# Feed-forwards of a hybrid decoder layer by Strassen's seven products

## The chip, the cores and the metric

One core of one Trainium2 chip runs the whole program. The metric is the device time of one execution in microseconds, the median of several runs. Lower is better.

## The reference

One layer of a decoder on 1024 prompt tokens and 64 sample tokens (8 sequences of 8), 1024 features wide, all in float32:

```python
def swiglu(x, w_in, w_out):                       # w_in 1024 x 5632, w_out 2816 x 1024
    gu = x @ w_in
    g, u = gu[..., :D_FF], gu[..., D_FF:]         # D_FF = 2816
    return (jax.nn.silu(g) * u) @ w_out

def layer(x, ...):
    x = x + 0.5 * swiglu(rmsnorm(x, norm_ffn1), ffn1_w_in, ffn1_w_out)
    mix, ... = token_mixing(rmsnorm(x, norm_mix), ...)
    x = x + mix
    x = x + 0.5 * swiglu(rmsnorm(x, norm_ffn2), ffn2_w_in, ffn2_w_out)
    return x, ...
# and a last rmsnorm over the features
```

The token mixing (a pooling branch and a state-space branch with their gates) is untouched by the change, apart from the buffers that it shares with the feed-forwards.

## The kernel before, in words

**Layout.** Everything is feature-major: a tile has 128 features on the partitions and tokens along the free dimension. The tokens are worked on in two parts, called halves: half 0 has 512 prompt tokens, half 1 has 512 prompt and 64 sample tokens, 576 together. A PSUM bank holds 512 float32 numbers, so half 1 is computed in two pieces of 288 columns.

**Precision.** Products run in the rounded format fp32r. Both operands are split into a rounded part (hi) and the exact remainder (lo), and each 128 x 128 block of weights takes part in three passes: hi x hi, hi x lo, lo x hi. `load_w` (lines 239 to 250) loads 512 columns of weights (tile `wraw`), rounds them on ScalarE (`wh`, line 248) and subtracts on VectorE (`wl`, line 249). `products` and `dense` run the three passes over all row blocks; line 140 is the one matmul line of all helpers.

**Feed-forward** (`ffn`). 22 hidden tiles of 128 features, in blocks of 3, 4, 4, 4, 4, 3. For a hidden tile, `dense` makes the gate part (PSUM tile `pg`) and the other part (`pu`) from 8 row blocks each; they are multiplied and split into hi and lo (`hb`, `hs`). After each block its hidden tiles are multiplied with the second weight (`po`) and added to the residual `x` in SBUF (line 431). The first block is done half by half, and so is the end of the last block. In the first feed-forward the products use x times the gain; the norm's factors (`rstd`) are multiplied onto the results (line 364), so that no product waits for them. In the second, `norm_split` makes the normalized operands ahead.

**Loading x** (`load_x`). Blocks of 128 tokens arrive token-major, are turned on TensorE against an identity (`ptx`, line 144), copied out of PSUM (line 466) and split.

**Order.** The kernel is written as a stream of dense products into which chains of small steps (norms, the state-space chunks, the final norm) are woven by an estimate of TensorE time (`tick`, `start`, `later`). The tile framework then orders each engine's instructions by priority and readiness, and gives out slots of the buffer pools. `hp[0]` raises the priority of the weights' splits. Loads and stores are issued from SyncE's queue (SP).

**Buffers.** One pool holds 58 slots of 128 x 576 (`act`), 3 of four times that size (`big`), 4 raw weight tiles and 4 each of `wh` and `wl`; 8 PSUM banks are shared by dense products (4) and all else (4).

**Between the feed-forwards** lies the mixing, half by half, which ends with the product `pwo` and, for half 0, a spill of x to DRAM. After the second feed-forward `final_head` and `final` turn x back to token-major, in two groups (six blocks of tokens, then three), and write the outputs.

Of the kernel before, what the change touches and what calls it, by code (L numbers as in the profile page):

```python
# [14 lines left out]
P = 128  # L15
# [19 lines left out]
FF_BLOCKS = (3, 4, 4, 4, 4, 3)   # hidden tiles per block of an FFN  # L35
N_ACT, N_BIG, N_PD = 58, 3, 4   # buffers: activation slots, 4-tile slots, PSUM banks of products
N_RAW, N_W = 4, 4   # weights as loaded, and split
# [12 lines left out]
X1_AT = 0.0  # L50
CONST_AT = 60.0
HP, HP_ST = 40, 0    # priorities of the weights' split and of the state update
N_PRE = 3            # weights ahead of x
# [3 lines left out]
def tile_hybrid_pool_ssd_macaron(  # L57
# [15 lines left out]
    pp = ctx.enter_context(tc.tile_pool(name="psum", bufs=8, space=bass.MemoryType.PSUM))  # L73
# [10 lines left out]

    def big(dt=F32, name="b"):
        return sp.tile([P, 4, 576], dt, tag="big", bufs=N_BIG, name=nm(name))

    def small(shape, name="s", bufs=2, dt=F32):
        return sp.tile(list(shape), dt, tag=name, bufs=bufs, name=nm(name))

    def psum(tag="ps", name="ps"):
        return pp.tile([P, 512], F32, tag=tag, bufs=N_PD if tag == "pd" else 8 - N_PD, name=nm(name))

# [1 line left out]
    # Chains of small steps (generators that yield how much TensorE time should pass before  # L95
    # their next step) are woven into the stream of dense products by TensorE time.
# [42 lines left out]
    def mm(out, lhsT, rhs, start=True, stop=True):  # L139
        T.matmul(out, lhsT, rhs, start=start, stop=stop)  # L140
        pe[0] += max(out.free_size(), 64) / 2400.0 * (1 if rhs.dtype == F32R else 4)
# [16 lines left out]
    # per-feature vectors arrive as rows and are turned into per-partition columns on PE  # L158
# [42 lines left out]
    xdtp = [cp.tile([P, 4, 2, P], F32, tag=f"xdtp{i}", name=f"xdtp{i}") for i in range(2)]  # L201
# [4 lines left out]
    def load_consts():  # L206
        """Constants that the mixing phase needs."""
# [11 lines left out]
        for t in xdtp:  # L219
            G.memset(t, 0.0)  # L220
# [42 lines left out]
    def dense(w, rk0, nk, c0, xs, tag="pd", name="pd"):  # L263
        """PSUM pieces of sum_k w[rk0+k, c0:c0+128]^T x[k]; xs: list of (half, hi, lo)."""
        out = banks(xs, tag, name)
        for kb in range(0, nk, 4):
            n4 = min(4, nk - kb)
            wh, wl = load_w(w, rk0 + kb, n4, c0)
            for kk in range(n4):
                products(out, wh, wl, kk, slice(0, P), xs, kb + kk, nk)  # L270
                tick()
        return out

    def dense2(w, rk0, c0, xs, tags=("pd", "pd"), name="pd"):
        """The same for two 128-column blocks of two 128-row blocks of w, one after the other."""
# [8 lines left out]
    def split(src, hi, lo, scale=1.0):  # L284
        """hi = f32r(src*scale), lo = src*scale - hi (exact)."""
# [17 lines left out]
    def rstd(tiles, h, count, out, pace=1.0):  # L303
        """Chain that fills out with rsqrt(mean(x^2)+eps) of feature-major x, on all partitions."""
# [17 lines left out]
        sm = small((P, 3, 5), "rsm", 2)  # L322
# [21 lines left out]
    def norm_split(xt, h, gi, out, pace=1.0):  # L344
        """Chain that fills out with the hi/lo parts of rmsnorm(x) of one half."""
# [25 lines left out]
    def h_tiles(nb):  # L371
        """hi and lo tiles of a block's hidden features: the big slots first, then the others."""
        room = []
        for _ in range(N_BIG):
            t = big(F32R, "hb")
            room += [t[:, j, :] for j in range(4)]
        while len(room) < 4 * nb:
            room.append(act((P, 576), F32R, "hs"))
        out = []
        for h in HALVES:  # L380
            t = [[room.pop(0)[:, : NTOK[h]] for _ in range(nb)] for _ in range(2)]
            out.append((h, t[0], t[1]))
        return out

    def ffn(xt, xs, wi, wo, before, after, rs=None, half=None, ends=((0,), (1,))):
# [3 lines left out]
        blocks, b0 = [], 0  # L389
        for nb in FF_BLOCKS:  # L390
            blocks.append((b0, nb))
            b0 += nb
        for i, (b0, nb) in enumerate(blocks):
            hp = h_tiles(nb)
            for grp in ((0,), (1,)) if i == 0 else (HALVES,):
                if i == 0:
                    before(grp[0])
                gx = [xs[h] for h in grp]
                for j in range(nb):
                    ff = b0 + j  # L400
                    first = rs is not None and i == 0 and j == 0
                    pg = dense(wi, 0, KD, ff * P, gx, "pd", "pg")
                    if first:
                        pu = dense(wi, 0, KD, FF + ff * P, gx, "ps", "pu")
                    sg = []
                    for h, pts in zip(grp, pg):
                        g_ = act((P, NTOK[h]), name="g")
                        if rs:
                            scaled(g_, pts, h, rs(h))
                            S.activation(g_, g_, AF.Silu)  # L410
                        else:
                            func(g_, pts, h, AF.Silu)
                        sg.append(g_)
                    if not first:
                        pu = dense(wi, 0, KD, FF + ff * P, gx, "ps", "pu")
                    for h, pts, g_ in zip(grp, pu, sg):
                        if rs:
                            u_ = act((P, NTOK[h]), name="u")
                            scaled(u_, pts, h, rs(h))
                            V.tensor_tensor(g_, g_, u_, op=ALU.mult)  # L420
                        else:
                            scaled(g_, pts, h, g_)
                        split(g_, hp[h][1][j], hp[h][2][j])
            last = i == len(blocks) - 1
            for gi, grp in enumerate(ends if last else (HALVES,)):
                for m in range(KD):
                    po = dense(wo, b0, nb, m * P, [(p, *hp[HALF_OF[p]][1:]) for p in grp], ("pd", "ps")[m % 2], "po")
                    for p, pts in zip(grp, po):
                        x_ = xt[HALF_OF[p]][m]
                        for pt, (a, b) in zip(pts, PIECES[p]):  # L430
                            V.scalar_tensor_tensor(x_[:, a:b], pt[:, : b - a], 0.5, x_[:, a:b],  # L431
                                                   op0=ALU.mult, op1=ALU.add)
                    if last and half and m == KD // 2 - 1:
                        half(gi)
                if last:
                    after(gi)

# [1 line left out]
    xt = [None, None]  # L439
    xs = [None, None]  # L440
# [820 lines left out]
```

## Time and profile before

| what | value |
|---|---|
| median of 3 runs | 3076.58 us (3070.76 to 3079.87) |
| profiled execution, first to last instruction | 3076.2 us |
| instructions | 46,636, of them 18,600 matmuls |
| TensorE (PE) | 3024.0 us busy, 98% |
| VectorE (DVE) | 1624.1 us, 53% |
| ScalarE (ACT) | 1028.7 us, 33% |
| GpSimd (POOL) | 56.4 us, 2% |
| DMA traffic | 261.10 MB, mean 85 GB/s |

PEld is TensorE's loading of weights, which runs beside its products. A stage's row has its window and length, then busy time and count of PE, PEld, DVE, ACT and POOL, then the granted TensorE clock (1.00 is full speed), the share of the DMA engines and GB/s. A row of the chain of waits has start, length, what ran, and how many in a row. A group's row has line, engine, operation, tiles and shapes with the count, then busy time, mean duration in ns, and the idle time of the engine before them with what ended it.

### The profile page before, as it was taken

How to read it: one execution, taken by the hardware profiler on the slowest of the kernel's cores; microseconds unless marked ns; L12 is line 12 of the kernel's file. 1: busy time of each engine (PE TensorE's matmuls, PEld its weight loads, DVE VectorE, ACT ScalarE, POOL GpSimd, SP SyncE). 2: the span in 40 equal slices, each digit the busy share in tenths (PEclk: the TensorE clock that was granted, in tenths of full speed). 3: DMA queues.
4: the chain of work that ended last, by engine and by line, in shares of the span. 5: the costliest groups of instructions: out<-in, count | busy, mean ns of one | idle time of the engine just before them, and what ended most of it. 6: DMA issues, size and time to landing. Idle time of an engine off the chain costs nothing.

```text
span 3076.2 us, 46636 instructions
## 1 busy us (share of the span) xinstructions
PE 3024.0 (98%) x18600; PEld 2750.7 (89%) x18600; DVE 1624.1 (53%) x3331; ACT 1028.7 (33%) x1967; POOL 56.4 (2%) x170
## 2 busy tenths in 40 slices
PE   6999999999999999999999999999999999999998
PEld 5999999999888888888999989999999999999997
DVE  5533333333673897777726886977773222322225
ACT  4221212121343665434425554543442212111113
POOL 0000000000000000000001110100000000000000
PEclk8999999999999999999999999999999999999999
DMA  4211111111434333435333434244432111111112
GB/s 132 67 45 45 45 45 45 45 45 43 130 97 124 113 103 92 117 117 183 91 102 95 123 104 119 88 139 124 145 113 64 44 45 45 45 45 45 45 41 98
DMA packets 439262, 261.10 MB, mean 85 GB/s; under 512 B 21795, under 2 KB 412066, under 8 KB 439036
## 3 DMA queue, kind: packets, MB, share of 16 engines
q1 hardware_dynamic: 439028, 258.11, 28.8%
q8 instruction: 146, 2.39, 0.3%
q14 instruction: 72, 0.59, 0.1%
q10 hardware_dynamic: 16, 0.00, 0.0%
HBM read 232.31 MB, written 25.97 MB: 84 GB/s over the span
## 4 chain that ended last, share of the span: by engine, by line
PE 92%; DVE 4%; DMA 2%; ACT 1%; issue 1%; SPq 0%; POOL 0%; ACTq 0%; DVEq 0%; POOLq 0%
PE pg L140 22%; PE pu L140 20%; PE po L140 17%; PE pc L140 8%; PE pz L140 6%; PE pso L140 5%; PE pwo L140 3%; PE pbp L140 3%; PE pyd L140 2%; PE pyos L140 1%; PE pst L140 1%; DMA bsel<-in_bsel_dram 1%; PE pyo L140 1%; PE pgm L140 1%; DVE wl L249 1%
## 5 line engine op out<-in xcount | busy, mean ns | idle before, releaser
L248 ACT ACTIVATE wh<-wraw 128x512 fp32r<-128x512 f32 (+1 forms) x708 | 440.2, 623 | 1643.8 <-PE pg L140 423.7
L249 DVE TENSOR_TENSOR wl<-wraw,wh 128x512 fp32r<-128x512 f32 (+1 forms) x708 | 479.1, 679 | 651.5 <-ACT wh L248 642.0
L140 PE MATMUL pg<-hi,wh 128*128 128x288 f32 (+1 forms) x1440 | 349.3, 331 | 15.4 <-ACT wh L248 15.4
L140 PE MATMUL po<-hb,wh 128*128 128x288 f32 (+2 forms) x1600 | 348.1, 339 | 0.0
L140 PE MATMUL pg<-lo,wh 128*128 128x288 f32 (+1 forms) x1440 | 346.3, 329 | 0.4 <-DVE lo L290 0.4
L140 PE MATMUL pg<-hi,wl 128*128 128x288 f32 (+1 forms) x1440 | 345.7, 328 | 0.0
L140 PE MATMUL pu<-hi,wh 128*128 128x288 f32 (+1 forms) x1248 | 293.9, 329 | 0.1
L140 PE MATMUL pu<-hi,wl 128*128 128x288 f32 (+1 forms) x1248 | 292.3, 328 | 0.0
L140 PE MATMUL pu<-lo,wh 128*128 128x288 f32 (+1 forms) x1248 | 292.2, 327 | 0.0
L140 PEld LDWEIGHTS pg<-hi,wh 128*128 128x128 f32 x1440 | 245.4, 189 | 38.0 <-ACT wh L248 16.3
L140 PEld LDWEIGHTS po<-hb,wh 128*128 128x128 f32 x1600 | 255.8, 188 | 19.6 <-ACT hb L286 0.3
L140 PEld LDWEIGHTS pg<-lo,wh 128*128 128x128 f32 x1440 | 245.3, 189 | 21.2 <-DVE lo L290 1.1
L140 PEld LDWEIGHTS pg<-hi,wl 128*128 128x128 f32 x1440 | 245.1, 189 | 20.7 <-DVE wl L249 0.4
L140 PE MATMUL po<-hb,wl 128*128 128x288 f32 (+3 forms) x1056 | 240.4, 328 | 0.0
L140 PEld LDWEIGHTS pu<-hi,wh 128*128 128x128 f32 x1248 | 211.8, 188 | 18.6 <-ACT wh L248 0.5
L140 PEld LDWEIGHTS pu<-hi,wl 128*128 128x128 f32 x1248 | 211.7, 188 | 17.7
L140 PEld LDWEIGHTS pu<-lo,wh 128*128 128x128 f32 x1248 | 211.7, 188 | 17.5
L140 PEld LDWEIGHTS po<-hb,wl 128*128 128x128 f32 x1056 | 178.6, 188 | 15.1
L431 DVE SCALAR_TENSOR_TENSOR x<-po,x 128x288 f32<-128x288 f32 (+3 forms) x240 | 108.7, 497 | 135.2 <-PE po L140 135.0
L140 PE MATMUL pc<-hi,wh 128*128 128x288 f32 (+1 forms) x576 | 162.8, 335 | 0.6 <-ACT craw L529 0.6
L140 PE MATMUL pc<-hi,wl 128*128 128x288 f32 (+1 forms) x576 | 159.7, 329 | 0.0
L140 PE MATMUL pc<-lo,wh 128*128 128x288 f32 (+1 forms) x576 | 158.6, 329 | 0.0
(283 smaller groups left out, 4608.6 us busy)
## 6 DMA issues: line engine op xcount, KB each, us to landing
wraw<-in_w_in_dram SPq DMA_DIRECT2D x260, 256.0 KB
wraw<-in_ffn_w_in_dram SPq DMA_DIRECT2D x200, 256.0 KB
wraw<-in_ffn_w_out_dram SPq DMA_DIRECT2D x64, 256.0 KB
ab<-acsd SPq DMA_DIRECT2D x64, 256.0 KB
wraw<-in_ssd_w_out_dram SPq DMA_DIRECT2D x64, 256.0 KB
wraw<-in_ffn_w_out_dram SPq DMA_DIRECT2D x48, 192.0 KB
wraw<-in_pool_w_out_dram SPq DMA_DIRECT2D x32, 256.0 KB
wraw<-in_w_o_dram SPq DMA_DIRECT2D x32, 256.0 KB
```

The costliest lines, as they stand in the source:

```text
L140: T.matmul(out, lhsT, rhs, start=start, stop=stop)
L248: S.activation(wh, raw, AF.Copy)
L249: V.tensor_tensor(wl, raw, wh.bitcast(F32), op=ALU.subtract)
L431: V.scalar_tensor_tensor(x_[:, a:b], pt[:, : b - a], 0.5, x_[:, a:b], op0=ALU.mult, op1=ALU.add)
```

## The change

The change touches both feed-forwards and what surrounds them.

**Seven products.** The weights of one hidden tile (gate and other part, each 8 row blocks) are taken as a 2 x 2 matrix of blocks: upper and lower four row blocks, gate and other columns. The inputs are taken in two by features (tiles 0 to 3 and 4 to 7) and two by tokens: columns 0 to n and n to 2n of a half, with n = 256 in half 0 and 288 in half 1. The form used is Winograd's variant of Strassen's: seven block products from four sums of weights (s1 to s4) and four of inputs. Seven input tiles per pair are kept, each holding its hi part in columns 0 to n and its lo part in n to 2n. The second product pairs hidden tiles of a block and pairs of column tiles in the same way. Blocks are now 6, 6, 6, 4 tiles. Sums of weights and of inputs, and a part of the accumulation, run on GpSimd.

**Hidden features through DRAM.** All 22 hidden tiles are made first and written to DRAM; the second product reads them back block by block, and makes a block's seven kinds of operands during the last pair of columns of the block before it (`behind`).

**x normalized by token, then turned.** `load_x` squares and sums the token-major rows, scales them, turns them, and applies the gain at the copy from PSUM. Raw x is loaded and turned a second time (`turn_x`) and spilled for the residual.

**Buffers.** Pools that belong to a stage are opened and closed (`open_stage`): PSUM is split 6 and 2 in the feed-forwards. Raw weights have 6 slots, `wh` and `wl` 3 each. The priority of the weights' splits is 300, not 40. The final norm's groups are the two halves (four blocks, then five).

The core of the diff:

```diff
+NPAIR = (256, 288)
+FF_BLOCKS = (6, 6, 6, 4)
+N_RAW, N_W = 6, 3
+N_X2, N_TMP, N_S, N_PDF = 12, 11, 4, 6
+N_APART = 4
+PRODUCTS = (("1", 0), ("2", 1), ("6", 0), ("5", 2), ("7", 0), ("3", 2), ("4", 0))
...
+HP, HP_ST = 300, 0
...
+    def wino_weights(w, ka, kb, nk, ca, cb, raws=None):
...
+        a11, a12, a21, a22 = raws
+        def add(a, b, op, name):
+            t = stage["p"].tile([P, 4 * P], F32, tag="wsum", bufs=N_S, name=nm(name))[:, : nk * P]
+            with tc.high_priority(hp[0]):
+                G.tensor_tensor(t, a, b, op=op)
+            return t
+        def parts(a):
...
+                S.activation(wh, a, AF.Copy)
+                V.tensor_tensor(wl, a, wh.bitcast(F32), op=ALU.subtract)
...
+        yield parts(a11)
+        yield parts(a12)
+        s1 = add(a21, a22, ALU.add, "s1")
+        s2 = add(s1, a11, ALU.subtract, "s2")
+        yield parts(s2)
+        yield parts(s1)
+        s3 = add(a11, a21, ALU.subtract, "s3")
+        yield parts(s3)
+        s4 = add(a12, s2, ALU.subtract, "s4")
+        yield parts(s4)
+        yield parts(a22)
...
+    def wino(weights, nk, xs, after, behind=None):
...
+        for (p, b), (wh, wl) in zip(PRODUCTS, weights):
+            for i, (h, X) in enumerate(xs):
...
+                for k in range(nk):
+                    x = X[p][k]
+                    for j, (W, c) in enumerate(((wh, 0), (wh, n), (wl, 0))):
+                        mm(out, W[:, k, :], x[:, c : c + n], start=new and k == 0 and j == 0, stop=k == nk - 1 and j == 2, free=True)
+                after(p, i, banks[i])
+                tick()
+            if behind:
+                behind(p)
+
+    def split_x(src, h):
+        n = NPAIR[h]
+        t = act((P, 576), F32R, "X")
+        S.activation(t[:, :n], src, AF.Copy)
+        V.tensor_tensor(t[:, n : 2 * n], src, t[:, :n].bitcast(F32), op=ALU.subtract)
+        return t
+
+    def combine(h, pairs, X):
...
+        def sub(out, a, b):
+            G.tensor_tensor(out, a, b, op=ALU.subtract)
+        for p, _ in PRODUCTS:
+            X[p] = []
+            for i, (a, b) in enumerate(pairs):
+                a1, a2, b1, b2 = a[:, :n], a[:, n : 2 * n], b[:, :n], b[:, n : 2 * n]
+                if p == "6":
+                    sub(a2, a2, a1)
+                    t2[i] = tmp(n, "t2")
+                    sub(t2[i], b2, a2)
+                elif p == "7":
+                    sub(a1, t2[i], a1)
+                elif p == "4":
+                    sub(b1, b1, t2[i])
+                X[p].append(split_x({"1": a1, "2": b1, "6": t2[i], "5": a2, "7": a1, "3": b2, "4": b1}[p], h))
+                yield
...
+    def ffn_in(wi, ff, xs, hd, raws=None, behind=None):
...
+            else:
+                V.tensor_tensor(g1, g1, A, op=ALU.mult)
+                G.tensor_tensor(g2, g2, o["t5"], op=ALU.mult)
+                dma(hd[h][ff], o["g"][:, : 2 * n])
...
+    def ffn_out(wo, k0, nk, m, xs, xt, behind=None):
...
+            if p in "167":
+                t = tmp(n)
+                S.activation(t, A, AF.Copy, scale=0.5)
+                o = {"1": a1, "6": a2, "7": b2}[p]
+                G.tensor_tensor(o, o, t, op=ALU.add)
+            else:
+                src, o = {"2": (B, a1), "5": (C, b2), "3": (C, a2), "4": (A, b1)}[p]
+                V.scalar_tensor_tensor(o, src, 0.5, o, op0=ALU.mult, op1=ALU.add)
...
+        for h in HALVES:
+            before(h)
+            for i, ff in enumerate(order[:N_APART]):
+                ffn_in(wi, ff, [(h, X[h])], hd, raws if h == 0 and i == 0 else None)
+        for ff in order[N_APART:-1]:
+            ffn_in(wi, ff, [(h, X[h]) for h in HALVES], hd)
...
+        ffn_in(wi, order[-1], [(0, X[0])], hd)
+        nk = FF_BLOCKS[0] // 2
+        nxt = stage_hidden(0, FF_BLOCKS[0])
...
+        ffn_in(wi, order[-1], [(1, X[1])], hd, behind=behind_in)
+        some(nxt[1], 7 * nk)
...
+        for bi, nb in enumerate(FF_BLOCKS):
...
+            for grp in ((0,), (1,)) if last else (HALVES,):
+                for m in range(0, KD, 2):
+                    roll = not last and m == KD - 2
+                    ffn_out(wo, b0, nk, m, [(h, H[h]) for h in grp], xt,
+                            behind=(lambda p: some(nxt[1], FF_BLOCKS[bi + 1] // 2)) if roll else None)
```

More of the change, by code (lines that the diff above doesn't have):

```diff
@@ L385, in ffn @@
[L385 to L391, printed above, removed]
-            b0 += nb
[L393 to L436, printed above, removed]
@@ L481, in before1 @@
+    ch, hn = {}, []
+    wi1 = ffn1_w_in[0]
+    raws1 = []
     def before1(h):
         if h == 0:
[L483 to L484 removed]
             finish(start(load_cols(0, nr0)))
[L486 to L487 removed]
+            c = start(load_x(0))
+            c.step()
+            raws1.extend(wino_raw(wi1, 0, 4, 4, 0, FF))
@@ L491, in before1, with turn, after1 @@
             finish(ch["x1"])
-            ch["r1"] = start(rstd(xt[1], 1, D, r1[1]))
             start(load_consts(), CONST_AT)
-    def rs1(h):
-        finish(ch[f"r{h}"])
-        return r1[h][0]
-    def after1(h):
+            def turn():
+                for h_ in HALVES:
+                    yield from turn_x(h_)
+            start(turn(), 30.0)
+    def after1(h, xt):
         if h == 0:
-            ch["hn"] = start(norm_split(xt[0], 0, i_gm, hn, HN_PACE))
+            ch["hn"] = start(norm_split([t[:, : NTOK[0]] for t in xt[0]], 0, i_gm, hn, HN_PACE))
         for m in range(KD):
-            dma(xspill[h][m], xt[h][m])
-    wi1 = ffn1_w_in[0]
-    ffn(xt, xs, wi1, ffn1_w_out[0], before1, after1, rs1)
+            dma(xspill[h][m], xt[h][m][:, : NTOK[h]])
+    st = open_stage("ffn1", N_PDF)
+    ffn(wi1, ffn1_w_out[0], X1, hdram, before1, after1, raws=raws1)
     finish(ch["hn"])
+    st.close()
+    st = open_stage("mix", N_PD)
+    xdtp = [stage["p"].tile([P, 4, 2, P], F32, tag=f"xdtp{i}", bufs=1, name=f"xdtp{i}") for i in range(2)]
+    for t in xdtp:
+        G.memset(t, 0.0)
     W = w_in[0]
```

284 lines of the change are left out of this document (209 added, 75 removed).

## The prediction, on record before the result

> **What bounds the kernel now.** I read the page first, then the stages, the chain of waits, the groups of instructions by form and, for GpSimd, the timeline.
>
> ```profile
> span 3076.2 us, 46636 instructions
> ...
> PE 3024.0 (98%) x18600; PEld 2750.7 (89%) x18600; DVE 1624.1 (53%) x3331; ACT 1028.7 (33%) x1967; POOL 56.4 (2%) x170
> ...
> PE 92%; DVE 4%; DMA 2%; ACT 1%; issue 1%; SPq 0%; POOL 0%; ACTq 0%; DVEq 0%; POOLq 0%
> PE pg L140 22%; PE pu L140 20%; PE po L140 17%; PE pc L140 8%; PE pz L140 6%; PE pso L140 5%; PE pwo L140 3%; PE pbp L140 3%; PE pyd L140 2%; PE pyos L140 1%; PE pst L140 1%; DMA bsel<-in_bsel_dram 1%; PE pyo L140 1%; PE pgm L140 1%; DVE wl L249 1%
> ```
>
> TensorE carries 92% of the chain, and most of that is the feed-forwards' products (pg, pu, po). The stages, with busy time and count of each engine, show where it is not full:
>
> ```profile
> 0.00:51.00 51.00, 28.29 (x117) 21.86 (x117) 19.57 (x41) 19.51 (x44) 2.66 (x10) 0.87 0.58 160
> 51.00:76.00 25.00, 23.52 (x115) 19.53 (x116) 18.93 (x52) 16.54 (x40) 0.00 (x0) 0.85 0.25 75
> 300.00:600.00 300.00, 300.00 (x1813) 273.38 (x1812) 100.15 (x182) 54.69 (x85) 0.00 (x0) 1.00 0.15 45
> 3040.00:3077.00 37.00, 23.19 (x167) 21.88 (x165) 25.71 (x72) 19.23 (x47) 0.00 (x0) 0.85 0.38 137
> ```
>
> Inside a feed-forward (300 to 600) PE has no idle time, DVE is a third busy, ACT a sixth, POOL does nothing, and the DMA engines are at 0.15. Only the first 76 us (24 us idle at a granted clock of 0.87) and the tail are loose. So time goes only if PE has fewer or shorter products, and the other engines have room to pay for it.
>
> **What one product costs.** The chain merges equal products, so a row divided by its count is the step from one to the next:
>
> ```profile
> 21.32 19.33 DMA bsel<-in_bsel_dram
> 43.72 7.10 DMA wraw<-in_ffn_w_in_dram
> 75.41 6.38 PE pg L140 x48
> 163.28 11.92 PE pu L140 x72
> 830.77 0.82 DVE x L431 x2
> 879.88 10.88 PE pu L140 x48
> 2267.07 5.46 PE pg L140 x24
> 3019.09 15.90 PE po L140 x90
> 3035.00 0.44 PE ptf L144 x4
> 3053.32 3.51 PE po L140 x24
> ```
>
> 288 columns: 6.38/48 = 133 ns. 512 columns: 10.88/48 = 227 ns. One 512 and two 288 together: 11.92/24 = 497 ns. The half with 512 and 256 columns: 15.90/45 = 353 ns a pair, so 256 cost at most 353-227 = 126 ns. Half of 512 would be 113, and a 128-column transpose still takes 0.44/4 = 110, so a shorter product would hit a floor there. I take 118 for 256 columns, with ends 113 and 126.
>
> Before: a feed-forward has 44x8 weight blocks in and 22x8 out, 528, times 3 passes, 1584 triples of 497 ns = 787 us. The feed-forwards run from about 12 to 832 us and from 2267 to 3057 us, so the first spends some 33 us on its start, the second 3 us.
>
> **After, on TensorE.** Seven products instead of eight, each in half-width pieces. In: 22 x 7 x 4 blocks x 3 passes x 2 halves = 3696 matmuls. Out: 11 pairs of row blocks x 4 pairs of columns x 7 x 3 x 2 = 1848. That is 5544 instead of 4752, half of 256 and half of 288 columns: 2772 x (118+133) = 696 us. Each feed-forward gains 91 us on PE, 182 us in all (210 at 113 ns, 138 at 126).
>
> **What it loads on the others.** The durations:
>
> ```profile
> L249 DVE TENSOR_TENSOR wl<-wraw,wh 128x512 fp32r<-128x512 f32 x660 | 452.6, 688 | 623.3 <-ACT wh L248 613.8 <-PE ph0T L144 2.5 <-DMA wraw<-in_pool_w_group_dram 2.5
> L249 DVE TENSOR_TENSOR wl<-wraw,wh 128x384 fp32r<-128x384 f32 x48 | 26.4, 552 | 28.2 <-ACT wh L248 28.2
> L431 DVE SCALAR_TENSOR_TENSOR x<-po,x 128x288 f32<-128x288 f32 x176 | 71.7, 449 | 3.4 <-PE po L140 3.3
> L248 ACT ACTIVATE wh<-wraw 128x512 fp32r<-128x512 f32 x660 | 415.0, 630 | 1541.8 <-PE pg L140 401.1 <-PE po L140 351.8 <-PE pu L140 322.8
> L368 ACT ACTIVATE g<-pg 128x288 f32<-128x288 f32 x44 | 15.5, 407 | 0.0
> L220 POOL MEMSET xdtp<- 128x1024 f32 x2 | 1.8, 952 | 0.0
> ```
>
> By count alone DVE and ACT have room. A hidden tile (21.1 us of PE for both halves): DVE 7 weight remainders of 0.69 and 8 evacuations of 0.45, 8.4 us; ACT 7 copies of 0.63 and 10 evacuations of 0.41, 8.5 us. Both hide, and so would they at twice the price.
>
> POOL is the unknown: four weight sums per tile, the X combinations, and three accumulations per half in the second product, all adds of two SBUF operands, of which before has none. Nearest row: the memset, 952 ns for 1024 elements, 0.93 ns an element, which only writes. One pass is the low end, three (two reads and the write in turn), 2.79 ns, the high end; I take two, 1.86: 0.95 us for 512, 0.71 for 384, 0.51 for a mean of 272. The Trainium skill (GPSIMD Engine Reference, section 3.1) gives 4497 ns for such an add of 2048 elements, 2.2 ns an element; at that price the sum below would come to about 3021 us.
>
> And POOL does not run beside DVE freely:
>
> ```profile
> 1692.68 1.28 DVE L249 TENSOR_TENSOR wl<-wraw,wh 128x512 fp32r<-128x512 f32 x2
> 1692.92 2.99 POOL L729 COPY crs<-hist 128x24 f32<-128x24 f32 x1 [3.29 <-DVE ct L743]
> 1693.88 0.75 DVE L746 SCALAR_TENSOR_TENSOR Cf<-cth,ct 128x576 f32<-128x576 f32 x1
> 1694.55 0.68 DVE L966 TENSOR_TENSOR hst<-hst,cd 128x512 f32<-128x512 f32 x1
> 1695.15 0.68 DVE L249 TENSOR_TENSOR wl<-wraw,wh 128x512 fp32r<-128x512 f32 x1
> 1695.76 0.68 DVE L968 TENSOR_TENSOR hst<-hst,pst 128x512 f32<-128x512 f32 x1
> 1695.84 0.18 POOL L728 COPY craw<-chist 128x3 f32<-128x3 f32 x1
> L729 POOL COPY crs<-hist x24: 200/560/3187, 1632.0 to 1949.2; 128x24 f32<-128x24 f32 x24
> ```
>
> A copy of 24 elements, 200 ns at best, took 2.99 us: it ended when the run of DVE instructions with two SBUF operands ended, while the next POOL copy ran at 0.18 us beside L968, whose second operand is in PSUM. So I add POOL's time and that of DVE's SBUF-SBUF instructions as on one port, and leave evacuations out. The Trainium skill (SBUF — State Buffer, "Who interferes with whom") calls this an exclusive lock, held for the whole instruction; the 2.99 us agrees. It speaks against this change, since the weight and X remainders on DVE are of that kind and POOL's sums feed them. DVE's hold I take by slope, (688-552)/128 = 1.06 ns an element: 0.54, 0.41 and 0.29 us for 512, 384 and 272.
>
> **Port time against PE time, stage by stage** (two-pass price):
>
> - Tile of one half (the first four of each): 7x0.54 + 4x0.95 + 0.5 = 8.1 us against 84 products, 9.9 or 11.2 us. Both halves: 8.6 against 21.1, hidden.
> - Second product, a pair of columns in a block of six: 7x0.41 + 4x0.71 + 6x0.51 = 8.8 against 15.8, hidden.
> - Behind a block the next one's X are made: 42 remainders (12.1) and 24 POOL subtractions (12.1). Half of the latter need only loaded tiles and can go earlier, leaving 18.2. X slots come free product by product, so all falls in this pair and the next one's: 17.6+18.2 = 35.8 against 31.6, 4 over. Two such; the third has four tiles and its second half has time: 0. About 9 with the round-up.
> - From first to second product: last tile of the second half and the first pair, 27.0 us, with 8.1+8.8+18.2 = 35.1: 8 over.
> - Last block (four tiles, halves apart): 5.3 against 5.0 or 5.6: 1.
> - Second half's X while the first runs alone: 28 remainders (8.6) and 16 subtractions (8.6), less slack 10.3: 7 over. In the second feed-forward the norm adds 15 DVE instructions of 576 (9.2): 16 over.
>
> **The rest.** Start: instead of splitting raw x, DVE and ACT wait for eight squares (0.63 each, behind loading), Newton's steps, scalings and transposes; the first product comes near 19 us, not 12.4, and the first tile's X (7.6+7.6 on the port) stretch it to some 23 us. But the small constant loads (19.33 us in SP's queue, weights landing 7.1 us later) hold PE until 51 us in any case; from 51 to 76 before had 23.5 us busy. I put the start at 16 worse, the 7 over included; ends 5 and 31. Raw x is turned again for the residual: 72 transposes of 0.11 = 8 us on PE, plainly added; its 72 evacuations hide. The mix's norm chain, 23 DVE instructions of 0.69 = 16 us, falls behind the last half's four pairs of 5.6, which hold 21 on the port already; its remainders are needed tile by tile, so I take 4 of it as uncovered (0 to 15). Two stage borders, where PSUM and tiles change hands: 2 each (0 to 5). Tail: five token blocks instead of three after the last product, 2 x 2 more pieces of 0.69 on DVE with their scaling: 4.
>
> Hidden activations go through DRAM: 88 DMAs of 256 or 288 KB per feed-forward, some 35 GB/s on top of 45 at a share of 0.15; nothing as long as weights lie ahead. On SP a store waits for the tile's last POOL product, and weight loads can stand behind it; six raw slots, half a tile more than in use, cover 10 us against POOL's longest wait of 3 here. Gone, it would cost up to 3 us a tile. In the mixing, three split slots instead of four: 0, ends 5 either way.
>
> **Sum.** First feed-forward: -91 + 8 + 16 + 8 + 9 + 1 + 4 + 2 = -43. Second: -91 + 16 + 8 + 9 + 1 + 4 + 2 = -51. Span 3076.2 - 94 = 2982 us. The median of the three runs is 3076.6, so the profiled execution stands for them.
>
> **Rivals.**
>
> POOL is cheap (one pass, 0.93 ns): rolls, transition and last block fit, start 10 and 4: -71 and -83, 2922 us. For it: evacuations and copies have a third of their engines left. Against: a memset reads nothing.
>
> POOL's adds become the bound (three passes, 2.79 ns). A tile of one half then needs 10.3 us of port against 9.9, a pair 11.7, a roll's rest 21.2: over by 13 per full roll and 5 for the third (31), 16 at the transition, 14 in the last block, 31 at each start. First: -91+8+31+16+31+14+8+2 = +19; second: -91+31+16+31+14+4+2 = +7: 3102 us, slower. It decides from about 2.6 ns an element. For it: one operand after the other through one port; the 2.99 us shows POOL getting in only when DVE pauses, so sums for the weights can also come late at a product. Against: two thirds of the PE time (joint tiles, ordinary pairs) keeps 4 us or more of slack a step even then.
>
> Weight loading bounds the half-width products: at 126 ns, 696 becomes 718 in each: 2982 + 44 = 3026 us. For it: PEld is at 273 of 300 us at 165 ns a step, and the step shrinks to 125. Against: the 110 ns floor lies under 118.
>
> That fewer columns are not what runs can be left out: the loops fix 5544 matmuls.
>
> **Chances.** Forecast 0.42, cheap POOL 0.22, POOL as bound 0.24, weight floor 0.12. Some 0.3% (9 us) is what a measurement of this kernel can tell from no change. Faster: nearly all of the first two, most of the last and a little of the third (a price under 2.6), 0.74; slower 0.21, same 0.05. The range leaves out the low end of the cheap case and the far end of the dear one: 2915 to 3095.
>
> **What would show it.** Right: some 20,200 matmuls; 128x256 and 128x288 at steps near 118 and 133; joint tiles of 21 us with PE idle nowhere; short PE gaps at the four block ends, with DVE waiting for POOL or the reverse. POOL adds of 512 near 1 us, longer where DVE is dense. Wrong: PE idle in joint tiles or ordinary pairs, waiting for wh or wl (then the sums or SP's order bind, not the rolls); adds over 1.4 us; a start over 20 us longer.

## The result

The changed kernel takes 3197.64 us (median of 4 runs, 3193.7 to 3201.72); the kernel before, on the same chip, 3076.09 us (3070.76 to 3079.87). The ratio is 1.040, 95% interval 1.038 to 1.042: slower by 122 us where 94 us less were forecast. The profiled execution has a span of 3191.9 us, 115.7 more than before.

The head of the page of the changed kernel, span first, then busy time, share and count of each engine:

```profile
span 3191.9 us, 54936 instructions
...
PE 2952.1 (92%) x20236; PEld 2788.6 (87%) x20236; DVE 2148.3 (67%) x4097; ACT 1440.6 (45%) x3188; POOL 960.6 (30%) x1066
...
L464 DVE TENSOR_TENSOR X<-hr,X 128x256 fp32r<-128x256 f32 (+1 forms) x264 | 194.1, 789 | 0.0
```

The 20,236 products are there. But TensorE, which was busy for 98% of the span, now is for 92%, and L464, the remainder of an input tile, takes 789 ns on the mean. Where the idle time lies is read from windows. In order: the start, in two rows; a stretch of joint hidden tiles; an ordinary pair of the second product; a rolled pair with the pair after it (a roll, from here on); the last block; the end of the second feed-forward.

```profile
0.00:51.00 51.00, 18.91 (x81) 15.91 (x81) 29.12 (x64) 22.83 (x62) 23.81 (x32) 0.90 0.37 101
51.00:140.00 89.00, 68.56 (x449) 64.87 (x450) 72.41 (x136) 53.68 (x138) 44.40 (x40) 0.83 0.35 105
300.00:500.00 200.00, 200.00 (x1588) 199.77 (x1587) 79.52 (x145) 76.40 (x164) 65.80 (x59) 1.00 0.28 87
613.90:629.70 15.80, 15.80 (x127) 15.80 (x127) 7.33 (x15) 5.73 (x13) 8.81 (x10) 1.00 0.17 51
630.00:681.00 51.00, 37.41 (x252) 36.45 (x251) 49.59 (x72) 24.45 (x68) 41.74 (x44) 0.83 0.31 97
816.00:886.00 70.00, 55.58 (x343) 48.04 (x343) 64.97 (x124) 35.38 (x92) 47.32 (x54) 0.95 0.41 127
3075.00:3175.00 100.00, 87.11 (x603) 82.27 (x602) 82.55 (x165) 55.72 (x153) 68.40 (x81) 0.91 0.22 68
```

The joint tiles run as forecast: 200/1588 = 126 ns a product, PE full, VectorE (DVE) at 0.40. The rolled pair does not: DVE is busy for 49.6 of 51 us, with only 72 instructions, 0.69 us each, and PE's granted clock falls to 0.83 between its stalls. DVE in that window by groups, then GpSimd (POOL):

```profile
L464 DVE TENSOR_TENSOR X<-hr,X 128x256 fp32r<-128x256 f32 (+1 forms) x36 | 27.9, 833 | 0.0
L416 DVE TENSOR_TENSOR wl<-wraw,wh 128x384 fp32r<-128x384 f32 x6 | 6.7, 1129 | 0.0
L546 DVE SCALAR_TENSOR_TENSOR x<-pw,x 128x288 f32<-128x288 f32 (+1 forms) x16 | 6.6, 430 | 0.8 <-PE pw L163 0.8
L416 DVE TENSOR_TENSOR wl<-s,wh 128x384 fp32r<-128x384 f32 x8 | 6.1, 764 | 0.0
L464 DVE TENSOR_TENSOR X<-t,X 128x256 fp32r<-128x256 f32 (+1 forms) x6 | 5.1, 857 | 1.3 <-ACT X L463 1.3
```

```profile
L543 POOL TENSOR_TENSOR x<-x,t 128x256 f32<-128x256 f32 (+1 forms) x12 | 11.1, 932 | 0.1
L474 POOL TENSOR_TENSOR hr<-hr 128x256 f32<-128x256 f32 (+1 forms) x6 | 6.1, 1030 | 0.0
L474 POOL TENSOR_TENSOR hr<-hr,t 128x256 f32<-128x256 f32 (+1 forms) x6 | 5.7, 992 | 0.0
L474 POOL TENSOR_TENSOR hr<-t,hr 128x256 f32<-128x256 f32 (+1 forms) x6 | 5.7, 975 | 0.0
L474 POOL TENSOR_TENSOR t<-hr,hr 128x256 f32<-128x256 f32 (+1 forms) x6 | 5.4, 926 | 0.0
L409 POOL TENSOR_TENSOR s<-wraw,wraw 128x384 f32<-128x384 f32 x4 | 4.3, 1082 | 8.4 <-DVE wl L416 8.4
```

The instructions with two operands in SBUF (L464, L416) are stretched to 0.76 to 1.13 us, while L546, whose one operand lies in PSUM, takes 430 ns. TensorE waits for that L546 all the same:

```profile
L163 PE MATMUL pw<-X,wh 128*128 128x288 f32 (+1 forms) x64 | 14.4, 325 | 7.7 <-DVE x L546 7.7
```

(TensorE in 636 to 662.) A product needs a PSUM bank; the bank is emptied by L546, which on DVE's queue stands behind the stretched remainders. In the rolls the adds off the path thus reach TensorE through the evacuations.

A stall costs more than its idle time. The roll takes 51.3 us for 31.6 us of products; 13.6 of the difference are idle. Most of the other 6 us is slower products: 46 of the 252 step at 207 to 240 ns, where 120 (256 columns) and 133 (288) are usual, while the granted clock is 0.5 (644.8 to 655.0 and 661.9 to 668.7), in and after gaps of 2.64 to 5.07 us. In the same roll of the first experiment below no gap is longer than 1.93 us, and the clock stays at 1.00. Over the whole run the clock stands at 0.5 for 238 us, against 60 in the kernel before, and TensorE is busy for 177 and 38 of these. Half of that busy time is lost, so slower products take some 70 us more than before, an estimate.

### The profile page after: what moved, and what is told of

The parts are those of the page before. It is cut to its first block, busy times and chain, and to the rows that moved or that the text cites. A ratio compares the mean times of both kernels' runs of the same rounds, so it can differ in the third digit from the quotient of the medians.

```text
span 3191.9 us, 54936 instructions
## 1 busy us (share of the span) xinstructions
PE 2952.1 (92%) x20236; PEld 2788.6 (87%) x20236; DVE 2148.3 (67%) x4097; ACT 1440.6 (45%) x3188; POOL 960.6 (30%) x1066
## 5 line engine op out<-in xcount | busy, mean ns | idle before, releaser
L163 PE MATMUL pw<-X,wh 128*128 128x256 f32 (+1 forms) x7392 | 1476.8, 299 | 140.1 <-DVE x L546 68.3
L163 PEld LDWEIGHTS pw<-X,wh 128*128 128x128 f32 x7392 | 1216.2, 198 | 158.9 <-DVE x L546 52.7
L163 PE MATMUL pw<-X,wl 128*128 128x256 f32 (+1 forms) x3696 | 1098.8, 298 | 24.5 <-DVE wl L416 24.0
L163 PEld LDWEIGHTS pw<-X,wl 128*128 128x128 f32 x3696 | 730.4, 198 | 34.6 <-DVE wl L416 33.2
L268 ACT ACTIVATE wh<-wraw 128x512 fp32r<-128x512 f32 x396 | 249.1, 630 | 496.4 <-PE pz L163 107.9
L416 DVE TENSOR_TENSOR wl<-s,wh 128x512 fp32r<-128x512 f32 (+2 forms) x376 | 274.7, 733 | 222.5 <-ACT wh L415 216.6
L269 DVE TENSOR_TENSOR wl<-wraw,wh 128x512 fp32r<-128x512 f32 x396 | 274.4, 694 | 220.2 <-ACT wh L268 205.8
L415 ACT ACTIVATE wh<-s 128x512 fp32r<-128x512 f32 (+2 forms) x376 | 212.6, 566 | 349.3 <-PE pw L163 304.7
L409 POOL TENSOR_TENSOR s<-wraw,wraw 128x512 f32<-128x512 f32 (+2 forms) x188 | 229.1, 1219 | 315.6 <-DVE wl L416 255.8
L416 DVE TENSOR_TENSOR wl<-wraw,wh 128x512 fp32r<-128x512 f32 (+2 forms) x282 | 220.3, 783 | 118.5 <-ACT wh L415 113.0
L464 DVE TENSOR_TENSOR X<-hr,X 128x256 fp32r<-128x256 f32 (+1 forms) x264 | 194.1, 789 | 0.0
L543 POOL TENSOR_TENSOR x<-x,t 128x256 f32<-128x256 f32 (+1 forms) x192 | 171.8, 899 | 49.2 <-ACT t L541 43.4
L546 DVE SCALAR_TENSOR_TENSOR x<-pw,x 128x256 f32<-128x256 f32 (+1 forms) x256 | 108.4, 434 | 55.7 <-PE pw L163 42.7
L409 POOL TENSOR_TENSOR s<-wraw,s 128x512 f32<-128x512 f32 (+2 forms) x94 | 117.5, 1250 | 79.3 <-issue 73.0
L409 POOL TENSOR_TENSOR s<-s,wraw 128x512 f32<-128x512 f32 (+2 forms) x94 | 112.0, 1191 | 81.5 <-issue 72.6
```

The source lines that it names most:

```text
L163: T.matmul(out, lhsT, rhs, start=start, stop=stop, skip_group_check=free)
L268: S.activation(wh, raw, AF.Copy)
L269: V.tensor_tensor(wl, raw, wh.bitcast(F32), op=ALU.subtract)
L409: G.tensor_tensor(t, a, b, op=op)
L415: S.activation(wh, a, AF.Copy)
L416: V.tensor_tensor(wl, a, wh.bitcast(F32), op=ALU.subtract)
```

## The experiments

Stage times below run from the first product of a stage to the first of the next, or to its own last one. A roll holds 31.7 us of products (252 of 126 ns), a last block 42.3, the eight first half-tiles 85. Ratios are to the kernel before on the same chip.

**All adds on VectorE.** The same edit in all four places where GpSimd adds or multiplies; the first of them:

```diff
-                G.tensor_tensor(t, a, b, op=op)
+                V.tensor_tensor(t, a, b, op=op)
```

> All of GpSimd's adds (weight sums, X subtractions, accumulation, the last multiply) are issued on VectorE instead; nothing else differs. In the changed kernel a roll (the pair of columns behind which the next block's X are made, and the pair after it) takes 51 us instead of 31.6, the last block 70, last tile of half 1 plus first pair 50, the two halves' first four tiles of the second feed-forward 116. Theory PORT (GpSimd's adds and VectorE's instructions with two SBUF operands exclude each other, so their times add): VectorE does the same adds in 0.41 to 0.69 us instead of 0.74 to 1.30 and waits for nobody; a roll needs 20.8 + 23.3 = 44 us, the last block some 50, last tile plus first pair 42, the first four tiles 94: about 110 us less in all, some 3085 us. Rival LOAD (VectorE's amount of work is what binds in these stretches; GpSimd helps by taking 1066 instructions off it): every stretch gets longer, rolls 60 and more, 3230 us or more.

Measured: 3096.18 us (4 runs), ratio 1.0063, interval 1.0048 to 1.0078. So 101 of the 122 us go with having these adds on GpSimd. The first four half-tiles, a roll, the last block:

```profile
26.00:102.00 76.00, 58.42 (x395) 53.90 (x394) 70.53 (x184) 53.70 (x143) 0.00 (x0) 0.89 0.34 97
600.00:640.50 40.50, 34.66 (x254) 32.26 (x253) 40.13 (x107) 24.69 (x69) 0.00 (x0) 1.00 0.22 65
761.00:831.00 70.00, 57.72 (x350) 49.53 (x348) 64.37 (x182) 38.01 (x101) 0.00 (x0) 0.92 0.40 126
```

The roll falls from 51 to 40.6 us although DVE now does 107 instructions in place of 72: one follows the other in 0.375 us. But DVE is full (40.13 of 40.5), so a second bound lies right beneath. The last block, for which PORT foresaw 50, is as long as before, with DVE at 64.37 of 70, and the first half-tiles have it at 70.53 of 76.

**No lock, the same work on GpSimd.** The remainders, of inputs and of weights alike, subtract zeros in PSUM instead of the rounded tile in SBUF, so no true low parts are computed; GpSimd's work stays. For the inputs:

```diff
-        V.tensor_tensor(t[:, n : 2 * n], src, t[:, :n].bitcast(F32), op=ALU.subtract)
+        V.tensor_tensor(t[:, n : 2 * n], src, stage["zz"][:, :n], op=ALU.subtract)
```

> VectorE's remainders of weights and X in the feed-forwards read a tile of zeros in PSUM as second operand instead of the rounded part in SBUF: same count, shapes and engines, GpSimd's work unchanged; the remainder's value is left out. One PSUM bank less for transposes. Theory PORT: with at most one SBUF operand VectorE no longer excludes GpSimd; a 256-wide remainder returns from 0.81 to 0.41 us and GpSimd's 256-wide add from 0.92 to 0.74; a roll is then GpSimd's own 36 us, last tile plus first pair 33, the last block 45, the first four tiles of the second feed-forward 88: about 3000 us. Rival SLOW POOL (GpSimd is just too slow, or its results come late in the queue): its work is the same, so rolls stay at 50 us and the time at 3200 within 20. Rival LOAD: the same, as VectorE's count is the same.

Measured: 3158.78 us in one run, a roll 47.4 us; its window, and three of GpSimd's groups in it, undisturbed now (three lines were added, so L412 and L477 are L409 and L474):

```profile
635.00:682.50 47.50, 36.67 (x255) 34.32 (x255) 29.84 (x74) 25.84 (x69) 34.36 (x44) 0.93 0.31 102
```

```profile
L412 POOL TENSOR_TENSOR s<-wraw,wraw 128x384 f32<-128x384 f32 x4 | 4.1, 1030 | 4.4 <-DVE wl L419 3.5 <-DMA wraw<-in_ffn_w_out_dram 0.9
...
L477 POOL TENSOR_TENSOR hr<-t,hr 128x288 f32<-128x288 f32 x3 | 2.4, 814 | 0.0
L477 POOL TENSOR_TENSOR hr<-hr 128x288 f32<-128x288 f32 x3 | 2.4, 809 | 0.5 <-DMA hr<-hd 0.5
```

DVE's 74 instructions fall from 0.69 to 0.40 us, yet the roll gains 3.6 us only. Without the lock the kernel is 39 us faster, in this one run; the other 62 of the 101 us, by difference, go with having to wait for GpSimd's own pace. PORT, by which a roll falls to 36 us, fell, and so did its rivals, by which the roll stays at 50 and the time within 20 of 3200. TensorE's longest gap in this roll shows how a slow add reaches it without any lock:

```profile
637.08 0.51 ACT L418 ACTIVATE wh<-s 128x384 fp32r<-128x384 f32 x1
645.29 0.42 DVE L467 TENSOR_TENSOR X<-t,zz 128x256 fp32r<-128x256 f32 x1 [3.11 <-POOL t L477]
649.67 0.45 DVE L467 TENSOR_TENSOR X<-t,zz 128x288 fp32r<-128x288 f32 x1 [0.33 <-POOL t L477]
650.04 0.55 DVE L419 TENSOR_TENSOR wl<-s,zz 128x384 fp32r<-128x384 f32 x1
650.64 0.58 PE L166 MATMUL pw<-X,wl 128*128 128x256 f32 x1 [4.96 <-DVE wl L419]
```

By the order of the products, the weight sum of L419 at 650.04 is the one that ScalarE rounds at 637.08. Its remainder stands in DVE's queue behind six remainders of inputs (645.29 to 649.67), each of which waits for a subtraction on GpSimd (L477). No run here tried another order in that queue.

**The accumulation off GpSimd.** Products 1, 6 and 7 are added to x by DVE straight from PSUM, not by a ScalarE copy and a GpSimd add.

```diff
-            if p in "167":
-                t = tmp(n)
-                S.activation(t, A, AF.Copy, scale=0.5)
-                o = {"1": a1, "6": a2, "7": b2}[p]
-                G.tensor_tensor(o, o, t, op=ALU.add)
...
+            src, o = {"1": (A, a1), "6": (A, a2), "7": (A, b2), "2": (B, a1), "5": (C, b2), "3": (C, a2), "4": (A, b1)}[p]
```

> Only the accumulation of products 1, 6 and 7 in the second product changes: VectorE adds them straight from PSUM as it does the other four, instead of a ScalarE copy and a GpSimd add (192 of each go, 192 VectorE instructions of 0.43 us with one SBUF operand come). Theory PORT: 6 x 0.77 us leave the port per pair, so a roll goes from 51 to 45 us, the last block from 70 to 45, last tile plus first pair from 50 to 45: some 80 us less, 3115 us. Rival LOAD: VectorE gets 192 x 0.43 = 83 us more work just where it is at 95%, so rolls and the last block grow by 4 to 8 us each: 3220 us or more.

Measured: 3189.55 us (4 runs), ratio 1.0371 (1.0353 to 1.0389); rolls 49.2, last block 72.3 and 67.6. That is 8 us less than the changed kernel, missed by both theories: what GpSimd is spared (192 adds), DVE takes on, and it is nearly full in these stages. The last tile of half 1 with the first pair even takes 54.9 instead of 50 us. A roll:

```profile
634.00:683.00 49.00, 36.09 (x253) 35.24 (x252) 44.71 (x84) 21.34 (x56) 30.52 (x32) 0.86 0.32 101
```

**The last block in one pass** (on all adds on VectorE; the final norm's two chains then start together):

```diff
-            for grp in ((0,), (1,)) if last else (HALVES,):
+            for grp in (HALVES,):
```

> Base: the kernel with all adds on VectorE (3096 us). The last block's pairs run for both halves together instead of half by half. There the last block still takes 70 and 76 us instead of 42, though the GpSimd adds are gone. Theory COVER (a product writes into a PSUM bank that must be emptied since the product before last; alone, a half's product of 6 matmuls lasts 0.72 us, too short for a 0.4 us evacuation with its queue, and each weight split serves one half): the block takes 48 us in both; as the norm chain and the output then start after it, some 15 us of that come back each time: 3075 us. Rival AMOUNT (VectorE's and ScalarE's work there, chains included, binds): block and chain together take as long as before, 3096 within 8.

Measured: 3066.42 us in one run; last block 47.0 and 50.7 us instead of 69.6 and 75.6. In more runs:

> The kernel with all adds on VectorE and the last block in one pass, now with enough rounds for an interval: 3066 was seen in one run, so 3064 to 3069, a ratio of 0.997 to the kernel before. By the rate of the products alone (787 to 696 us in each feed-forward) it would be 2894; what it leaves of that is in the first tiles, the rolls and the last block.

Measured: 3070.45 us (11 runs), ratio 0.998 (0.9972 to 0.9989), just above the range. Its last block:

```profile
764.00:811.00 47.00, 45.34 (x339) 43.13 (x338) 44.94 (x123) 27.84 (x71) 0.00 (x0) 1.00 0.40 129
```

DVE has 19.4 us less to do there, of which the weights' remainders and sums of the second half, made only once now, are nearly all. It is still at 0.96. So this run alone doesn't tell a short cover for each bank from too much work on VectorE; the next does.

**The small block first** (blocks of 4, 6, 6, 6; halves apart in the last; on all adds on VectorE):

> Base: all adds on VectorE. Blocks of 4, 6, 6, 6 hidden tiles instead of 6, 6, 6, 4: the last block, done half by half, now has products of 9 matmuls (1.06 to 1.2 us). COVER: it takes 66 to 70 us for six tiles (ideal 63) where four took 70 to 76; the first block of four 42 to 50; 25 us less in each feed-forward, 3048 us. AMOUNT: VectorE needs 7.8 us a pair and half, 62 in all, plus the 16 of the chain: 80 us or more, 3085 us.

Measured: 3092.6 us in one run; the last block, with products half as long again, takes 86.0 and 90.6 us against 63 of products. It loses 23 and 28 us, where the block of four lost 27 and 33:

```profile
747.00:833.00 86.00, 77.45 (x511) 71.33 (x510) 79.26 (x195) 46.55 (x108) 0.00 (x0) 0.90 0.40 121
```

So more cover for each bank cures little, and COVER's 66 to 70 us are out. AMOUNT fits better, though the block takes still longer than its 80 us: with the halves apart the weights' work is done twice, on VectorE above all (79.26 of 86 us) and on ScalarE. The two were not told apart.

**No sums of inputs** (the subtractions at L474 left out, so that the seven operands are plain quarters of the input; on all adds on VectorE):

> Base: all adds on VectorE. The subtractions that combine the inputs (X) are left out; the products, splits and everything else stay. Theory AMOUNT for the rolls (VectorE's count in two pairs, 44 us of it, sets the 40.6 us that a roll takes): without 24 x 0.35 us a roll takes 33, last tile of half 1 plus first pair 33 instead of 40, the first eight half-tiles of the second feed-forward 92 instead of 104: some 70 us less, 3026 us. Rival SLOTS (X slots that come free product by product, or the order in the queues, set the rolls): rolls stay above 38, 3080 us.

Measured: 3015.78 us in one run, 80 less than with them on VectorE; rolls 34.2 us, near AMOUNT's 33 and below the 38 of SLOTS, with DVE still full:

```profile
585.00:620.00 35.00, 33.75 (x260) 32.66 (x259) 34.29 (x90) 24.24 (x69) 0.00 (x0) 1.00 0.40 119
```

**No first norm** (squares, Newton's steps and the scaling of token-major x left out, so that the first feed-forward's input is not normalized; on all adds on VectorE):

> Base: all adds on VectorE. The first norm's factors are left out (squares, Newton's steps and the scaling of token-major x); loading, turning, gains and X stay. It prices the norm before the turn. If the norm ahead of the first product is the cost: first product near 16 us instead of 26, the first eight half-tiles end near 125 instead of 149: 3072 us. If the start is bound by making X and by loads: the first product is 8 us earlier, but the eight half-tiles still end after 142: 3090 us.

Measured: 3086.68 us in one run; the first product at 21 instead of 26 us, the eight half-tiles done at 137 instead of 149. Normalizing first costs 12 us, between the expectations.

**Only product 6's subtractions on GpSimd** (on the last block in one pass):

> The last block in one pass and, of all the adds, only the subtractions for product 6 on GpSimd, with everything else on VectorE. In the changed kernel a roll has 24 subtractions on GpSimd, 20 us of work in one in-order queue; here 8 of them are left there, about 8 x 0.77 = 6 us, and VectorE has the other 16 at 0.4 to 0.45 us, about 7 us instead of 10 with all 24. Theory QUEUE (GpSimd's work costs by its amount in one queue, and a few adds that lie early are hidden): a rolled pair of tiles takes 36 to 37 us instead of 40.6 (all on VectorE) and 50 (all on GpSimd); two such pairs and the transition in each of two feed-forwards give 6 x 4 = 24 us: 3040 to 3045. Theory LOCK (each add of GpSimd holds VectorE's two-operand instructions up by 0.4 us and more): the 8 adds cost VectorE what they spare it, rolls stay at 40 to 41, time 3064 to 3070.

Measured: 3074.63 us (11 runs), ratio 0.9992 (0.9983 to 1.0001), 4 us slower than without, missed by both theories. The first feed-forward's rolls take 38.3 and 40.4 us instead of 40.6 and 41.9, but other stages lose it again: the first four half-tiles of the second feed-forward 57.2 instead of 48.5. Even a few adds on GpSimd give nothing here.

**The mixing.** It is 14.6 us longer in the changed kernel, where no product of it changed. First the kernel before with the changed buffers and priority:

```diff
-N_RAW, N_W = 4, 4   # weights as loaded, and split
+N_RAW, N_W = 6, 3   # weights as loaded, and split
...
-HP, HP_ST = 40, 0    # priorities of the weights' split and of the state update
+HP, HP_ST = 300, 0    # priorities of the weights' split and of the state update
```

> The kernel before with the changed kernel's weight buffers and priority only (6 raw and 3 split slots instead of 4 and 4, priority 300 instead of 40). It asks where the mixing's 14.6 us (1434.9 to 1449.5) come from. If buffers and priority: the mixing here takes 1445 us or more, the feed-forwards as before within 3 us, 3087 us. If pools, spills or neighbours: the mixing stays at 1435 within 3, 3077 us.

then with the three split buffers alone,

> The kernel before with one number changed: 3 buffers instead of 4 for split weights, with 4 raw buffers and the split's priority as before. The run with 6 raw, 3 split and the changed priority had its mixing stage at 1452 us instead of 1435. Theory BUFFERS (a fourth split weight is what let the projections run ahead): mixing 1447 to 1453, time 3088 to 3094. Theory PRIORITY (the split's higher priority puts it ahead of the mixing's own work on VectorE and ScalarE): mixing 1433 to 1438, time 3075 to 3080.

then the best version so far with the old priority in the mixing alone:

```diff
+    hp[0] = 40
     c, _ = mix_half(0, hn[0], prep_b)
...
     st = open_stage("ffn2", N_PDF)
+    hp[0] = HP
```

> All adds on VectorE, the last block in one pass, and the weights' split priority put back to 40 for the mixing stage alone (300 in both feed-forwards). Theory PRIORITY (the changed priority of the weights' split costs the mixing stage its 12 to 18 us): mixing 1434 to 1440 us instead of 1447 to 1453, time 3056 to 3060, a ratio of 0.994 to the kernel before. Theory BUFFERS (6 raw and 3 split buffers instead of 4 and 4 cost it): mixing stays at 1447 to 1453, time 3066 to 3072.

The mixing by windows, from its first product to the end of its last. The kernel before:

```profile
831.90:2266.80 1434.90, 1419.90 (x8910) 1290.43 (x8910) 1040.12 (x2198) 666.15 (x1318) 53.25 (x156) 0.99 0.40 116
```

The changed kernel:

```profile
890.40:2339.90 1449.50, 1421.31 (x8909) 1291.07 (x8909) 1047.49 (x2198) 665.09 (x1329) 62.90 (x181) 0.99 0.40 115
```

The kernel before with 6 and 3 buffers and a priority of 300 (3092.99 us, one run):

```profile
828.50:2280.80 1452.30, 1424.16 (x8910) 1291.33 (x8909) 1045.51 (x2199) 666.43 (x1318) 38.80 (x156) 0.99 0.40 114
```

With three split buffers alone (3084.54 us, one run; this time and the stage lie just above what PRIORITY foresaw):

```profile
834.20:2272.90 1438.70, 1418.51 (x8910) 1286.87 (x8909) 1040.79 (x2198) 665.13 (x1318) 53.83 (x156) 0.99 0.40 116
```

The best version with 40 in the mixing:

```profile
824.50:2263.60 1439.10, 1419.67 (x8908) 1287.26 (x8909) 1042.98 (x2216) 662.77 (x1325) 56.19 (x161) 0.99 0.40 116
```

The split's priority is most of it: 1439 us with 40 for it, 1447 to 1456 with 300 in the runs with all adds on VectorE, 8 to 17 us; three buffers alone add 4, in one run. The whole takes 3058.75 us (5 runs), ratio 0.9944 (0.9931 to 0.9958): 0.6% faster than the kernel before, of the 3% that were forecast. One group shows where part of it goes, the state-space output product, first in the kernel before:

```profile
L140 PE MATMUL pso<-yh,wh 128*128 128x288 f32 (+1 forms) x384 | 113.4, 348 | 6.0 <-ACT acc L1048 2.8 <-ACT yh L286 2.4 <-ACT craw L529 0.7
```

with the changed buffers and priority:

```profile
L140 PE MATMUL pso<-yh,wh 128*128 128x288 f32 (+1 forms) x384 | 115.7, 352 | 11.8 <-ACT acc L1048 4.1 <-DVE acc L1050 3.8 <-ACT yh L286 3.1
```

and with the priority put back:

```profile
L163 PE MATMUL pso<-yh,wh 128*128 128x288 f32 (+1 forms) x384 | 114.3, 348 | 5.5 <-ACT acc L1290 2.2 <-ACT yh L306 2.1 <-ACT craw L771 0.8
```

TensorE waits there for evacuations (acc) and operands (yh) on ScalarE and VectorE, and splits that go ahead of them make it wait longer.

## Why the prediction was wrong

The terms of its sum, as extra time in each feed-forward (first, second):

| term | forecast | measured |
|---|---|---|
| products | -91, -91 | -91, -91 |
| start | 16, 16 | 39, 28 |
| x turned again | 8, - | 8, - |
| first to second product | 8, 8 | 23, 23 |
| rolls | 9, 9 | 43, 45 |
| last block | 1, 1 | 28, 27 |
| border, norm chain, tail | 6, 6 | 4, 11 |
| mixing, once | 0 | 15 |

Measured, these sum to 54 + 43 + 15 = 112 of the 115.7 us; the rest lies scattered. Of the 210 us between the forecast span and the measured one, the rolls make 70, the last blocks 53, the starts 35, the way from first to second product 30, the mixing 15.

**Right: TensorE's part, while it runs without stalls.** 126 ns a product against 125.5, with 120 for 256 columns and 133 for 288; joint tiles and ordinary pairs hide their adds. The rival of a weight-loading floor at 126 ns for 256 columns is out. But PEld is busy for 199.77 of 200 us there; whether it is what holds 256 columns at 120 and not 118 is not shown.

**The step that failed: GpSimd's price.** "Two passes, 1.86 ns an element" gave 0.51 us for 272 elements and 0.71 for 384. Undisturbed they are 0.81 (288) and 1.03 (384): (1030-809)/96 = 2.3 ns an element and some 0.15 us for each instruction, which the sum had left at nothing. For small tiles that constant is a fifth of the price. The 2.2 ns an element of the Trainium skill (GPSIMD Engine Reference, section 3.1) is near this slope, for a tile of 2048 elements. The rival of three passes came nearest in sign and time (3102), in part by luck: its 2.79 ns make 0.80 us for 288 and 1.07 for 384, close to the 0.81 and 1.03 measured, because a slope that is too steep stands in for the constant. The cheap one is out; from the terms it names, its two sums come to -67 and -81 instead of -71 and -83, on which nothing rests.

**A term that the sum left at nothing: slower products after a stall.** All 5544 products of a feed-forward are taken at full clock. The stretches at half clock cost some 70 us more than in the kernel before, by the estimate above; the table has them inside the stages where they occur.

**Two smaller steps of the roll.** "Half of the latter ... can go earlier" was not so: all 24 subtractions lie in the window of the two pairs (6 + 6 + 6 + 6 in L474's groups). And VectorE "by slope", 0.29 and 0.41 us, was too cheap. In a stream of such instructions the next starts some 0.08 us before the record of the last ends (three at 438 ns in 1.03 us), so the step is 0.34 to 0.37 us for these sizes and 0.47 for 384:

```profile
611.76 0.56 DVE L416 TENSOR_TENSOR wl<-wraw,wh 128x384 fp32r<-128x384 f32 x1
612.23 1.13 DVE L464 TENSOR_TENSOR X<-t,X 128x256 fp32r<-128x256 f32 x3
613.26 1.16 DVE L474 TENSOR_TENSOR t<-hr,hr 128x288 f32<-128x288 f32 x3
```

(VectorE in a roll with all adds on it.) With these prices the prediction's own sum is 42 x 0.35 + 14 x 0.47 = 21 us of VectorE and 36 x 0.8 + 8 x 1.03 = 37 of GpSimd, 58 on one port, where it had 35.8; 51 were measured, some of them at half clock. So the port model named the right stages, and is too strict as a sum.

**What the model left out** is that each engine also has a queue of its own. Without the lock the roll still takes 47.4 us; 9.0 of TensorE's 10.8 us of gaps there end with weight remainders, which in the longest gap stand behind remainders that wait for GpSimd. And VectorE has its evacuations besides: with all adds on it, 42 + 14 remainders, 16 evacuations, 36 input sums and accumulations and 8 weight sums, 116 instructions, make 116 x 0.375 = 43 us against 31.7 of products. None of the ways tried of sharing these adds between the two engines fits them into a roll.

**Last block.** "5.3 against 5.0 or 5.6" suffers from the same prices: 7 remainders of 0.34 and 7 adds of some 0.76 on GpSimd are 7.7 us for each pair of a half, against 5.3 of products, eight times: 19 us over, 28 measured. But this is not the whole cause: with no add on GpSimd the block takes 70 and 76 us all the same, and 47 and 51 once the halves share the weights' work. The prediction had that work twice in its count, but not the norm chain's beyond 4 us, nor the price of VectorE's evacuations. And TensorE's gaps in the changed kernel's block end mostly with weight remainders (10.2 of 14.4 us), not with evacuations.

**Start.** Of the 39 us in the first feed-forward, 20 go with GpSimd's adds and 12 with the norm put in front; the prediction had both mechanisms and less than half of their size, and its own sign of being wrong, a start over 20 us longer, is there. The 7 that stay were not traced further.

**Mixing.** Taken at 0 with ends of 5, and only the buffers were weighed; the priority, in the same diff, was not.

## What to carry to other kernels

When work moves off TensorE, sum each other engine's instructions, with the constant part of each and the evacuations, over the shortest stage and not over the mean: here TensorE's gain ends where VectorE's queue fills, and the wait shows up on what stands last in that queue, a PSUM evacuation or a weight's remainder. Adds of two SBUF operands on GpSimd beside VectorE work of the same kind were no free lane here: VectorE did the same adds in half the time, and the kernel was 101 us faster for it. A global priority for one helper is a change to every stage that calls it.

## What was not expected of the hardware

VectorE's smallest instructions were held up too. GpSimd's weight sums in the start of the changed kernel, and VectorE's Newton steps on 4 elements a partition (start, length, engine, line):

```profile
14.40 1.26 POOL L409 TENSOR_TENSOR s<-wraw,wraw 128x512 f32<-128x512 f32 x1 [12.94 <-DMA wraw<-in_ffn_w_in_dram]
15.73 1.27 POOL L409 TENSOR_TENSOR s<-s,wraw 128x512 f32<-128x512 f32 x1
16.97 1.26 POOL L409 TENSOR_TENSOR s<-wraw,wraw 128x512 f32<-128x512 f32 x1
```

```profile
14.55 1.13 DVE L652 TENSOR_SCALAR xss<-xss 128x4 f32<-128x4 f32 x1
15.72 0.17 DVE L316 TENSOR_SCALAR xss<-xss 128x4 int32<-128x4 int32 x1
15.92 1.11 DVE L317 TENSOR_SCALAR xss<-xss 128x4 f32<-128x4 f32 x1
16.95 0.15 DVE L319 TENSOR_TENSOR xss<-xss 128x4 f32<-128x4 f32 x1
17.13 1.11 DVE L320 TENSOR_TENSOR xss<-xss 128x4 f32<-128x4 f32 x1
```

Each one that starts inside an add ends with it, 1.1 us instead of 0.16; those that slip in between two adds take 0.15 to 0.17. Even an instruction with one tensor operand (L652, L317) waits. The Trainium skill (SBUF — State Buffer, "Who interferes with whom") has it that such scalar operations too can take the shared port and then block fully; this trace agrees, with 1.13 us.
